# An encoder trunk whose odd mixer gets its weight parts split ahead of time and kept in DRAM scratch

## The chip, the cores and the metric

The kernel runs on one core of a Trainium2 chip. The metric is the device time of one execution in microseconds (us), as the median of several runs. A core has a matrix engine (TensorE, PE in the profile, with its weight loads as PEld), a vector engine (DVE), a scalar engine (ACT), GpSimd (POOL) and a queue that issues DMA transfers (SP). Each engine works through its own instructions strictly in the order in which the program was built; engines wait for each other by semaphores. SBUF is the on-chip memory with 128 partitions, PSUM the small memory that the matrix engine writes, in 8 banks, and DRAM holds inputs, outputs and scratch.

## The reference

Two layers work on x of 512 tokens by 1024 channels, in float32. Each layer is

```
x = x + 1/2 * post1(SwiGLU_1(pre1(x)))
x = x + post2(Mixer(pre2(x)))
x = x + 1/2 * post3(SwiGLU_2(pre3(x)))
```

with RMS norms pre and post, and SwiGLU(h) = (silu(h @ w_gate) * (h @ w_up)) @ w_down with an inner width of 2816. The mixer of layer 0 (the even one) has pooling and windowed attention. The mixer of layer 1 (the odd one) projects h to 4128 columns (od_w_in), runs a convolution of 31 taps over 512 gated channels (the glu pair), a layer norm, a short convolution of 4 taps over 2048 channels (xbc), and a state-space scan in both directions over 16 heads in 4 groups and 4 chunks of 128 tokens; the scan's result is gated by silu(z), normed, joined with the convolution's and projected back (od_w_out).

## The kernel before

The stages run one after the other: feed-forward (0,0), even mixer, feed-forward (0,1), feed-forward (1,0), odd mixer, feed-forward (1,1). Every large product is computed with three matmuls (`mm3`): each operand is given as hi, its rounding to the matmul type fp32r, and lo, the remainder, and hi*hi + hi*lo + lo*hi are added up in a PSUM bank. So each weight has to be split before use.

`Stream` does this for all weights in the order in which they are used. A weight block is some 1 MB, laid out as 128 partitions by 2048 floats; SP loads it into one of 3 buffers (tile `raw`, `RAW_BUFS`). A block has two parts of 128 x 1024. `pump` splits the next part: ACT rounds it into a tile `whi` (line 103), DVE subtracts and writes `wlo` (line 104). whi and wlo are rings of 6 tiles each (`RING`); `get` hands out the next part, `put` gives a ring slot back after its matmuls have been issued and pumps the next split. A raw buffer is loaded again when both its parts are split. A feed-forward stage has 33 blocks: three groups of gate, up and down blocks (names f_g, f_u, f_y in PSUM). The odd mixer has 23: for each of four groups g a block for the gated channels (psum od_ab), one for the scan's B and C (od_bc) and one for the scan's input (od_xs), once a small one for the step sizes (od_dt), four for the gate (od_z), and six of od_w_out (odo_y).

A stage begins with six parts (`first`, `second`): half of the tokens with all six, then the other half, so that the last norm of the stage before can end meanwhile; six ring slots are taken at that time.

In the odd mixer smaller work is woven between the projection's matmuls. DVE computes conv31, 31 instructions for each group (tile `od_ca`, lines 878 and 883), the short convolutions conv4 (`od_cv_B`, `od_cv_C`, `od_cv_x`, line 896), and the chain of the step sizes (`od_dv` to `od_dt`, `od_nacs`, `od_wdec`, `od_rhl`, lines 917 to 970). For each group the scan takes the weighted inputs `od_xw` (line 1007), states `od_st..` (PE) and `od_h` (DVE, lines 1019 and 1020), the scores `od_sc` (PE), their exponentials `od_E` (ACT, line 1046), `od_m` (DVE, lines 1050 and 1051), then `od_yd` and `od_yo` (PE), which DVE adds to `od_y` (lines 1071, 1080, 1082).

What is issued when follows from coroutines with hand-set delays (`Gen.run`), and a scheduling layer below it sets the order of each engine's instructions by its own estimate of when their inputs are ready. So a change of DVE's work in one place can move instructions of any engine.

Of the kernel before, what the change touches and what calls it, by code (L numbers as in the profile page):

```python
# [7 lines left out]
F32 = mybir.dt.float32  # L8
# [4 lines left out]
ALU = mybir.AluOpType  # L13
AX = mybir.AxisListType

P = 128
# [35 lines left out]
LNWAIT = (3500, 2500, 8000)  # L52
SSDWAIT = 2950
CONVWAIT = 5000
DWB, LNG, LNB, CVB, CVW = 0, 4, 8, 12, 28


class Stream:

    def __init__(self, g, blocks):
        self.g = g
        self.blocks = blocks
        self.parts = [(b, j) for b, blk in enumerate(blocks) for j in range(len(blk["parts"]))]
        self.raw, self.done = {}, {}
        self.nraw = self.nsplit = self.pos = 0
        self.live_raw = self.live = 0

    def _load(self, bufs=RAW_BUFS):  # L70
        while self.nraw < len(self.blocks) and self.live_raw < bufs:
            blk = self.blocks[self.nraw]
            t = self.g.raw.tile([P, 2048], F32, tag="raw", name=f"raw{self.nraw}")
            a, b = blk["shape"]
            v = t[:, : a * b].rearrange("p (a b) -> p a b", b=b)
            if self.nraw == 0:
                for h in range(0, b, b // 2):
                    self.g.nc.sync.dma_start(out=v[:, :, h:h + b // 2], in_=blk["src"][:, :, h:h + b // 2])
            elif "srcs" in blk:
                for dst, src in blk["srcs"]:  # L80
                    self.g.nc.sync.dma_start(out=v[dst], in_=src)
            else:
                self.g.nc.sync.dma_start(out=v, in_=blk["src"])
            self.raw[self.nraw] = v
            self.nraw += 1
            self.live_raw += 1

    def pump(self, room=RING):

        g, nc = self.g, self.g.nc  # L90
        self._load()
        while self.nsplit < len(self.parts) and self.live < room:
            b, j = self.parts[self.nsplit]
            if b not in self.raw:
                break
            sl = self.blocks[b]["parts"][j]
            src = self.raw[b][:, sl[0], sl[1]]
            n0, n1 = src.shape[1], src.shape[2]
            h = g.whi.tile([P, 1024], F32R, tag="whi", name=f"whi{self.nsplit}")
            l = g.wlo.tile([P, 1024], F32R, tag="wlo", name=f"wlo{self.nsplit}")  # L100
            hv = h[:, : n0 * n1].rearrange("p (a b) -> p a b", b=n1)
            lv = l[:, : n0 * n1].rearrange("p (a b) -> p a b", b=n1)
            g.later(nc.scalar.copy(out=hv, in_=src), 0)  # L103
            g.later(nc.vector.tensor_tensor(out=lv, in0=src, in1=hv.bitcast(F32), op=ALU.subtract), 1)  # L104
            self.done[self.nsplit] = (hv, lv)
            self.nsplit += 1
            self.live += 1
            if j == len(self.blocks[b]["parts"]) - 1:
                del self.raw[b]
                self.live_raw -= 1  # L110
                self._load()

    def get(self, key):
        b, j = self.parts[self.pos]
        assert self.blocks[b]["key"] == key[:-1] and j == key[-1], (self.blocks[b]["key"], j, key)
        if self.pos not in self.done:
            self.pump()
        r = self.done.pop(self.pos)
        self.pos += 1
        return r  # L120

    def put(self, n=1, pump=True):

        self.live -= n
        if pump:
            self.pump()


def full(n):
    return slice(0, n)  # L130


def ffn_blocks(d, l, i):
    out = []
    f0 = 0
    wg = d["ffn_w_gate"][l, i].rearrange("(k p) f -> p k f", p=P)
    wu = d["ffn_w_up"][l, i].rearrange("(k p) f -> p k f", p=P)
    wd = d["ffn_w_down"][l, i].rearrange("(j p) n -> p j n", p=P)
    for n in FGROUPS:
        for f in range(f0, f0 + n, 2):  # L140
            for nm, w in (("g", wg), ("u", wu)):
                out.append(dict(key=(nm, l, i, f // 2), src=w[:, :, f * P:(f + 2) * P], shape=(KC, 256),
                                parts=[(full(KC), slice(0, 128)), (full(KC), slice(128, 256))]))
        for f in range(f0, f0 + n, 2):
            out.append(dict(key=("d", l, i, f // 2), src=wd[:, f:f + 2, :], shape=(2, 1024),
                            parts=[(slice(0, 1), full(1024)), (slice(1, 2), full(1024))]))
        f0 += n
    return out
# [78 lines left out]
class Gen:  # L227
# [599 lines left out]
    def odd(self):  # L827
# [6 lines left out]
        with ExitStack() as es:  # L834
# [39 lines left out]
            def conv31(g, t):  # L874
# [5 lines left out]
                for i, k in enumerate(k for k in range(31) if k != 15):  # L880
# [4 lines left out]
                    if i % CONVN == CONVN - 1:  # L885
                        yield CONVWAIT

# [362 lines left out]
    def build(self, stages):  # L1250
        nc, tc, d = self.nc, self.tc, self.d
        with ExitStack() as es:
# [11 lines left out]
            self.xl = xp.tile([P, KC, S], F32R, tag="xl", name="xl")  # L1264

            seq = [s for s in ALL if s in stages]
            blocks = []
            for s in seq:
                blocks += ffn_blocks(d, s[1], s[2]) if s[0] == "f" else odd_blocks(d) if s[1] else even_blocks(d)
            self.st = Stream(self, blocks)  # L1270

            def row(s, which):
                l, j = s[1], {"f": (0, 4), "m": (2,)}[s[0]][s[2] if s[0] == "f" else 0] + (which == "post")
# [84 lines left out]
```

## Time and profile before

| | |
|---|---|
| median of 3 runs (lowest to highest) | 2049.24 us (2048.62 to 2052.99) |
| the profiled execution's own time | 2049.17 us |
| its span, first to last instruction | 2047.4 us |
| busy: PE, DVE, ACT, POOL | 2002.0 (98%), 968.1 (47%), 754.3 (37%), 67.7 us (3%) |
| moved by DMA, mean rate | 185.79 MB, 91 GB/s (HBM written 2.10 MB) |
| casts into whi, subtractions into wlo | 329 each, 345.0 us on ACT and 400.9 us on DVE |

The page's own share of PE, 98%, is an average over stages that differ, so the table of stretches below is to be read first. A row of it gives for each engine the busy time within the stretch and the number of instructions in brackets; PEclk is the clock that TensorE was granted, as a share of full speed. In a timeline the brackets at a row's end tell how long the engine had been idle before, and whose result ended that. The last chain is the path of work, followed back from the kernel's end, on which every piece waited for the one before it.

### The profile page before, as it was taken

The numbers are of one execution on the slowest core, as the hardware profiler recorded it, in microseconds if no ns is written. First come the engines' busy times: TensorE is split into PE (matmuls) and PEld (weight loads), VectorE is DVE, ScalarE is ACT, GpSimd is POOL, SyncE is SP. The second block draws the span as 40 slices with busy tenths as digits, with TensorE's granted clock in tenths as the row PEclk, the third lists the DMA queues.
The fourth block names the chain that finished last, engine by engine and source line by source line (L and its number), as shares of the span: only waits on it lengthen the run. The fifth ranks groups of instructions, "written<-read, shape, count | busy, mean of one in ns | idle before, by whom it ended". The sixth has DMA issues, their size and how long they took to land.

```text
span 2047.4 us, 24628 instructions
## 1 busy us (share of the span) xinstructions
PE 2002.0 (98%) x10257; PEld 1693.1 (83%) x10257; DVE 968.1 (47%) x1436; ACT 754.3 (37%) x1242; POOL 67.7 (3%) x94
## 2 busy tenths in 40 slices
PE   8999999999989999999999999998899999999998
PEld 7888888988888888889888888986778889888886
DVE  5323333667453233336323333699898553323334
ACT  5222222576343222224323222465654433232222
POOL 1000000111100000001000000100000010000000
PEclk9999999999999999999999999998899999999999
DMA  7322332330223233322333233232111223233221
GB/s 238 108 88 98 103 100 65 78 100 22 83 96 110 85 101 103 96 89 92 115 103 98 88 103 103 48 106 59 42 62 63 93 71 115 93 103 101 84 83 41
DMA packets 154871, 185.79 MB, mean 91 GB/s; under 512 B 18480, under 2 KB 137864, under 8 KB 154760
## 3 DMA queue, kind: packets, MB, share of 16 engines
q1 hardware_dynamic: 154760, 184.22, 28.7%
q8 instruction: 80, 1.31, 0.3%
q14 instruction: 31, 0.25, 0.0%
HBM read 182.11 MB, written 2.10 MB: 90 GB/s over the span
## 4 chain that ended last, share of the span: by engine, by line
PE 90%; DVE 6%; ACT 2%; POOL 1%; issue 1%; DMA 0%; SPq 0%; POOLq 0%; DVEq 0%; ACTq 0%
PE f_u L299 23%; PE f_g L299 23%; PE f_y L299 23%; PE od_z L299 2%; PE odo_y L299 2%; PE od_bc L299 2%; PE od_ab L299 2%; PE evo_y L299 1%; PE ev_av L299 1%; PE od_xs L299 1%; DVE od_ca L883 1%; PE od_yd L299 1%; PE ev_s L299 1%; PE od_sc L299 1%; PE ev_q L299 1%
## 5 line engine op out<-in xcount | busy, mean ns | idle before, releaser
L103 ACT CAST whi<-raw 128x1024 fp32r<-128x1024 f32 x329 | 345.0, 1052 | 981.2 <-PE f_g L299 323.6
L104 DVE TENSOR_TENSOR wlo<-raw,whi 128x1024 fp32r<-128x1024 f32 x329 | 400.9, 1221 | 630.2 <-ACT whi L103 625.1
L299 PE MATMUL f_g<-xl,whi 128*128 128x512 f32 (+1 forms) x832 | 296.7, 357 | 1.7 <-DVE xl L363 1.4
L299 PE MATMUL f_g<-xh,whi 128*128 128x512 f32 (+1 forms) x832 | 297.2, 357 | 0.6 <-ACT xh L362 0.6
L299 PE MATMUL f_g<-xh,wlo 128*128 128x512 f32 (+1 forms) x832 | 296.4, 356 | 0.0
L299 PE MATMUL f_u<-xh,whi 128*128 128x512 f32 (+1 forms) x768 | 286.5, 373 | 0.2 <-DVE xl L363 0.2
L299 PE MATMUL f_u<-xl,whi 128*128 128x512 f32 (+1 forms) x768 | 286.0, 372 | 0.0
L299 PE MATMUL f_u<-xh,wlo 128*128 128x512 f32 (+1 forms) x768 | 286.0, 372 | 0.0
L299 PE MATMUL f_y<-whi,f_hh 128*128 128x512 f32 x704 | 274.4, 390 | 0.0
L299 PE MATMUL f_y<-whi,f_hl 128*128 128x512 f32 x704 | 273.9, 389 | 0.0
L299 PE MATMUL f_y<-wlo,f_hh 128*128 128x512 f32 x704 | 273.9, 389 | 0.0
L527 DVE TENSOR_TENSOR f_hf<-f_sg,f_u 128x512 f32<-128x512 f32 x88 | 60.6, 689 | 250.5 <-PE f_u L299 249.9
L299 PEld LDWEIGHTS f_g<-xl,whi 128*128 128x128 f32 x832 | 157.2, 189 | 24.9 <-DVE xl L363 1.9
L299 PEld LDWEIGHTS f_g<-xh,whi 128*128 128x128 f32 x832 | 157.2, 189 | 23.8 <-ACT xh L362 1.3
L299 PEld LDWEIGHTS f_g<-xh,wlo 128*128 128x128 f32 x832 | 157.2, 189 | 22.4
L299 PEld LDWEIGHTS f_u<-xh,whi 128*128 128x128 f32 x768 | 145.7, 190 | 25.3 <-DVE xl L363 0.4
L299 PEld LDWEIGHTS f_u<-xl,whi 128*128 128x128 f32 x768 | 145.6, 190 | 24.8
L299 PEld LDWEIGHTS f_u<-xh,wlo 128*128 128x128 f32 x768 | 145.5, 189 | 24.9
L299 PEld LDWEIGHTS f_y<-whi,f_hl 128*128 128x128 f32 x704 | 132.2, 188 | 27.4
L299 PEld LDWEIGHTS f_y<-wlo,f_hh 128*128 128x128 f32 x704 | 132.2, 188 | 27.3
L299 PEld LDWEIGHTS f_y<-whi,f_hh 128*128 128x128 f32 x704 | 132.2, 188 | 27.2
L883 DVE SCALAR_TENSOR_TENSOR od_ca<-od_glu,od_dww,od_ca 128x497 f32<-128x497 f32 (+14 forms) x120 | 88.4, 737 | 0.2
(378 smaller groups left out, 2509.4 us busy)
## 6 DMA issues: line engine op xcount, KB each, us to landing
raw<-ffn_w_up SPq DMA_DIRECT2D x44, 1024.0 KB, 5.3
raw<-ffn_w_down SPq DMA_DIRECT2D x44, 1024.0 KB, 4.9
raw<-ffn_w_gate SPq DMA_DIRECT2D x43, 1024.0 KB, 5.3
raw<-od_w_in SPq DMA_DIRECT2D x16, 512.0 KB, 5.4
raw<-od_w_in SPq DMA_DIRECT2D x8, 1024.0 KB, 5.4
raw<-od_w_out SPq DMA_DIRECT2D x6, 1024.0 KB, 4.9
raw<-ev_w_in SPq DMA_DIRECT2D x3, 1024.0 KB, 5.1
raw<-ev_w_in SPq DMA_DIRECT2D x12, 256.0 KB, 4.5
```

The source lines that it names most:

```text
L103: g.later(nc.scalar.copy(out=hv, in_=src), 0)
L104: g.later(nc.vector.tensor_tensor(out=lv, in0=src, in1=hv.bitcast(F32), op=ALU.subtract), 1)
L299: self.seq(bank, self.nc.tensor.matmul(reg, a, b, start=start, stop=stop, skip_group_check=True))
L527: nc.vector.tensor_tensor(out=h, in0=sg, in1=pu, op=ALU.mult)
L883: V.scalar_tensor_tensor(out=o[:, lo:hi], in0=t[:, lo + sh:hi + sh], scalar=dww[:, k * 4 + g:k * 4 + g + 1], in1=o[:, lo:hi], op0=ALU.mult ...
```

## The change

The blocks of the odd mixer appear twice in the stream now. Their first appearance lies among the feed-forward blocks of the three stages ahead, before the blocks number 6, 9, 13, 16, 19, 22, 25 and 28 of each (`KEEP`; 8, 8 and 7 blocks). There they are loaded and split as any other block, and SP then stores hi and lo of each part into DRAM scratch (tiles k..h and k..l). No matmul uses them there; `_pass` gives their ring slots back as soon as all parts ahead of them have been given back. In the odd mixer, their second appearance, a part needs no raw buffer, no cast and no subtraction: SP loads hi and lo from scratch straight into whi and wlo (line 114 of the new kernel). `_load` skips these blocks, so the raw buffers go on to the blocks of the last feed-forward stage.

```diff
--- before.py
+++ after.py
@@ -52,10 +52,13 @@
 LNWAIT = (3500, 2500, 8000)
 SSDWAIT = 2950
 CONVWAIT = 5000
+KEEP = (6, 9, 13, 16, 19, 22, 25, 28)
 DWB, LNG, LNB, CVB, CVW = 0, 4, 8, 12, 28
 
 
 class Stream:
...
@@ -63,13 +66,16 @@
         self.g = g
         self.blocks = blocks
         self.parts = [(b, j) for b, blk in enumerate(blocks) for j in range(len(blk["parts"]))]
-        self.raw, self.done = {}, {}
-        self.nraw = self.nsplit = self.pos = 0
+        self.raw, self.done, self.kept = {}, {}, {}
+        self.nraw = self.nsplit = self.pos = self.put_to = 0
         self.live_raw = self.live = 0
 
     def _load(self, bufs=RAW_BUFS):
         while self.nraw < len(self.blocks) and self.live_raw < bufs:
             blk = self.blocks[self.nraw]
+            if "split" in blk:
+                self.nraw += 1
+                continue
             t = self.g.raw.tile([P, 2048], F32, tag="raw", name=f"raw{self.nraw}")
             a, b = blk["shape"]
             v = t[:, : a * b].rearrange("p (a b) -> p a b", b=b)
@@ -91,26 +97,46 @@
         self._load()
         while self.nsplit < len(self.parts) and self.live < room:
             b, j = self.parts[self.nsplit]
-            if b not in self.raw:
+            blk = self.blocks[b]
+            if "split" not in blk and b not in self.raw:
                 break
-            sl = self.blocks[b]["parts"][j]
-            src = self.raw[b][:, sl[0], sl[1]]
-            n0, n1 = src.shape[1], src.shape[2]
+            n0, n1 = (sl.stop - sl.start for sl in blk["parts"][j])
             h = g.whi.tile([P, 1024], F32R, tag="whi", name=f"whi{self.nsplit}")
             l = g.wlo.tile([P, 1024], F32R, tag="wlo", name=f"wlo{self.nsplit}")
             hv = h[:, : n0 * n1].rearrange("p (a b) -> p a b", b=n1)
             lv = l[:, : n0 * n1].rearrange("p (a b) -> p a b", b=n1)
-            g.later(nc.scalar.copy(out=hv, in_=src), 0)
-            g.later(nc.vector.tensor_tensor(out=lv, in0=src, in1=hv.bitcast(F32), op=ALU.subtract), 1)
             self.done[self.nsplit] = (hv, lv)
             self.nsplit += 1
             self.live += 1
-            if j == len(self.blocks[b]["parts"]) - 1:
+            last = j == len(blk["parts"]) - 1
+            if "split" in blk:
+                for t, k in zip((h, l), self.kept.pop((blk["key"], j))):
+                    nc.sync.dma_start(out=t[:, :n0 * n1].bitcast(F32), in_=k)
+                continue
+            sl = blk["parts"][j]
+            src = self.raw[b][:, sl[0], sl[1]]
+            g.later(nc.scalar.copy(out=hv, in_=src), 0)
+            g.later(nc.vector.tensor_tensor(out=lv, in0=src, in1=hv.bitcast(F32), op=ALU.subtract), 1)
+            if "keep" in blk:
+                self.kept[blk["key"], j] = [g.keep.tile([P, n0 * n1], F32, tag=f"k{self.nsplit}{x}", name=f"k{self.nsplit}{x}") for x in "hl"]
+                for t, k in zip((h, l), self.kept[blk["key"], j]):
+                    nc.sync.dma_start(out=k, in_=t[:, :n0 * n1].bitcast(F32))
+                self._pass()
+            if last:
                 del self.raw[b]
                 self.live_raw -= 1
                 self._load()
 
+    def _pass(self):
+
+        while self.put_to < self.nsplit and "keep" in self.blocks[self.parts[self.put_to][0]]:
+            self.put_to += 1
+            self.live -= 1
+
     def get(self, key):
+        while "keep" in self.blocks[self.parts[self.pos][0]]:
+            self.done.pop(self.pos, None)
+            self.pos += 1
         b, j = self.parts[self.pos]
         assert self.blocks[b]["key"] == key[:-1] and j == key[-1], (self.blocks[b]["key"], j, key)
         if self.pos not in self.done:
@@ -122,12 +148,27 @@
     def put(self, n=1, pump=True):
 
         self.live -= n
+        self.put_to += n
+        self._pass()
         if pump:
             self.pump()
 
 
 def full(n):
     return slice(0, n)
+
+
+def keep(blocks, ffns):
+
+    todo = list(blocks)
+    for f in ffns:
+        for i in reversed(KEEP[:len(todo)]):
+            f.insert(i, None)
+        for i, b in enumerate(f):
+            if b is None:
+                f[i] = dict(todo.pop(0), keep=True)
+    assert not todo
+    return [dict(b, split=True) for b in blocks]
 
 
 def ffn_blocks(d, l, i):
@@ -1264,10 +1305,10 @@
             self.xl = xp.tile([P, KC, S], F32R, tag="xl", name="xl")
 
             seq = [s for s in ALL if s in stages]
-            blocks = []
-            for s in seq:
-                blocks += ffn_blocks(d, s[1], s[2]) if s[0] == "f" else odd_blocks(d) if s[1] else even_blocks(d)
-            self.st = Stream(self, blocks)
+            lists = {s: ffn_blocks(d, s[1], s[2]) if s[0] == "f" else odd_blocks(d) if s[1] else even_blocks(d) for s in seq}
+            lists["m", 1] = keep(lists["m", 1], [lists[s] for s in seq[:seq.index(("m", 1))] if s[0] == "f"])
+            self.keep = pool("keep", 1, space=bass.MemoryType.DRAM)
+            self.st = Stream(self, [b for s in seq for b in lists[s]])
 
             def row(s, which):
                 l, j = s[1], {"f": (0, 4), "m": (2,)}[s[0]][s[2] if s[0] == "f" else 0] + (which == "post")
```

On DVE, in the odd mixer's first group, around the first od_wdec (it needs od_acs, a product of PE; od_dz and od_dq belong to the step sizes, od_cv_B is a short convolution, od_rhl feeds the scores), there stood:

```order
L952 TENSOR_TENSOR od_wdec<-od_acs 128x128
L896 SCALAR_TENSOR_TENSOR od_cv_B_10625<-od_bc_10592,od_cols,od_cv_B_10625 128x511
L936 TENSOR_TENSOR od_dz<-od_dz,od_de 128x128
L896 SCALAR_TENSOR_TENSOR od_cv_B_10625<-od_bc_10592,od_cols,od_cv_B_10625 128x511
L937 TENSOR_SCALAR od_dq<-od_dz 128x128
L956 TENSOR_TENSOR od_wdec<-od_wdec,od_dt 128x128
L938 RECIPROCAL od_dq<-od_dq 128x128
L970 TENSOR_TENSOR od_rhl_10205<-od_acsh,od_jm 32x512
L939 SCALAR_TENSOR_TENSOR od_dz<-od_dz,od_dq 128x128
L970 TENSOR_TENSOR od_rhl_10205<-od_acsh,od_jm 32x512
L940 SCALAR_TENSOR_TENSOR od_nacs<-od_dz,od_nacs 128x128
```

and there stands now:

```order
L977 TENSOR_TENSOR od_dz<-od_dz,od_de 128x128
L937 SCALAR_TENSOR_TENSOR od_cv_B_11018<-od_bc_10985,od_cols,od_cv_B_11018 128x510
L978 TENSOR_SCALAR od_dq<-od_dz 128x128
L937 SCALAR_TENSOR_TENSOR od_cv_B_11018<-od_bc_10985,od_cols,od_cv_B_11018 128x511
L979 RECIPROCAL od_dq<-od_dq 128x128
L937 SCALAR_TENSOR_TENSOR od_cv_B_11018<-od_bc_10985,od_cols,od_cv_B_11018 128x511
L980 SCALAR_TENSOR_TENSOR od_dz<-od_dz,od_dq 128x128
L993 TENSOR_TENSOR od_wdec<-od_acs 128x128
L981 SCALAR_TENSOR_TENSOR od_nacs<-od_dz,od_nacs 128x128
L1011 TENSOR_TENSOR od_rhl_10611<-od_acsh,od_jm 32x512 x2
L1011 TENSOR_TENSOR od_rhl_10612<-od_acsh,od_jm 32x512 x2
L924 SCALAR_TENSOR_TENSOR od_ca_10585<-od_glu_10983,od_dww,od_ca_10585 128x498
```

The reciprocal and its neighbours, and the convolution steps, have moved ahead of od_wdec; the wlo that stood three rows ahead of it is gone.

On DVE, a little later, from the first od_y that adds an od_yd (first chunk of the first group) on, there stood:

```order
L1071 TENSOR_TENSOR od_y<-od_y,od_yd_10820 128x256
L883 SCALAR_TENSOR_TENSOR od_ca_10178<-od_glu_10267,od_dww,od_ca_10178 128x498
L1050 TENSOR_TENSOR od_m_10803<-od_E_10798,od_E_10793 128x512
L883 SCALAR_TENSOR_TENSOR od_ca_10178<-od_glu_10267,od_dww,od_ca_10178 128x497
L1051 TENSOR_TENSOR od_m_10803<-od_m_10803,od_cb_10540 128x512
L1082 TENSOR_TENSOR od_y<-od_y,od_yo_10830 128x256
L104 TENSOR_TENSOR wlo_10835<-raw_10440,whi_10834 128x1024
L896 SCALAR_TENSOR_TENSOR od_cv_x_10840<-od_xs_10736,od_cols,od_cv_x_10840 128x510
L878 TENSOR_SCALAR od_ca_10179<-od_glu_10590,od_dww,od_cols 128x512
L896 SCALAR_TENSOR_TENSOR od_cv_x_10840<-od_xs_10736,od_cols,od_cv_x_10840 128x511
L883 SCALAR_TENSOR_TENSOR od_ca_10179<-od_glu_10590,od_dww,od_ca_10179 128x497
L896 SCALAR_TENSOR_TENSOR od_cv_x_10840<-od_xs_10736,od_cols,od_cv_x_10840 128x511
```

and there stands now:

```order
L1112 TENSOR_TENSOR od_y<-od_y,od_yd_11210 128x256
L937 SCALAR_TENSOR_TENSOR od_cv_x_11228<-od_xs_11126,od_cols,od_cv_x_11228 128x511
L1123 TENSOR_TENSOR od_y<-od_y,od_yo_11220 128x256
L1060 TENSOR_TENSOR od_h_11283<-od_h_11213,od_etot 128x256
L924 SCALAR_TENSOR_TENSOR od_ca_10585<-od_glu_10983,od_dww,od_ca_10585 128x502
L1061 TENSOR_TENSOR od_h_11283<-od_h_11283,od_yd_11280 128x256
L924 SCALAR_TENSOR_TENSOR od_ca_10585<-od_glu_10983,od_dww,od_ca_10585 128x503
L1091 TENSOR_TENSOR od_m_11193<-od_E_11188,od_E_11183 128x512
L1121 TENSOR_TENSOR od_yo_11291<-od_yo_11281,od_eacs 128x512
L1092 TENSOR_TENSOR od_m_11193<-od_m_11193,od_cb_10936 128x512
L924 SCALAR_TENSOR_TENSOR od_ca_10585<-od_glu_10983,od_dww,od_ca_10585 128x504
L1060 TENSOR_TENSOR od_h_11346<-od_h_11283,od_etot 128x256
```

A wlo and several od_ca have left; od_h and the next chunks' od_m have come nearer to the od_y. A second wlo, 15 rows further on, is gone too.

On SP, at the end of feed-forward (1,0), where the odd mixer's first weights are fetched (raw from od_w_in; k.. are scratch tiles), there stood:

```order
L83 DMA raw_9335<-ffn_w_down 128x2x1024
L83 DMA raw_9403<-ffn_w_down 128x2x1024
L83 DMA raw_9471<-ffn_w_down 128x2x1024
L81 DMA raw_9539<-od_w_in 128x8x128 x2
L81 DMA raw_9608<-od_w_in 128x8x128 x2
L83 DMA raw_9677<-od_w_in 128x8x256
L83 DMA raw_9898<-od_w_in 128x8x32
L81 DMA raw_9977<-od_w_in 128x8x128 x2
L81 DMA raw_9988<-od_w_in 128x8x128 x2
L845 DMA od_pb<-ssm_dt_bias 128x32
```

and there stands now:

```order
L89 DMA raw_9887<-ffn_w_down 128x2x1024
L89 DMA raw_9955<-ffn_w_gate 128x8x256
L89 DMA raw_10023<-ffn_w_up 128x8x256
L89 DMA raw_10091<-ffn_w_gate 128x8x256
L114 DMA wlo_10299<-k13l 128x1024
L114 DMA whi_10298<-k13h 128x1024
L114 DMA whi_10308<-k14h 128x1024
L114 DMA wlo_10309<-k14l 128x1024
L114 DMA whi_10318<-k21h 128x1024
L114 DMA wlo_10319<-k21l 128x1024
L114 DMA whi_10385<-k22h 128x1024
L114 DMA wlo_10386<-k22l 128x1024
```

The three raw buffers take blocks of feed-forward (1,1), and behind them come the loads of hi and lo, two for each part.

## Rows read from the trace of the kernel before

**Rows 1.** by stretch, us: feed-forward block (1,0), odd mixer's middle. Columns: first row.

```profile
core 0: us, PE busy (x) PEld busy (x) DVE busy (x) ACT busy (x) POOL busy (x), PEclk, DMA share, GB/s
...
942.00:1307.00 365.00, 365.00 (x1765) 308.72 (x1764) 140.62 (x165) 111.30 (x152) 7.34 (x9) 1.00 0.31 98
...
1350.00:1580.00 230.00, 213.52 (x1078) 172.71 (x1076) 209.49 (x368) 132.65 (x261) 0.00 (x0) 0.93 0.20 60
```

**Rows 2.** timeline of PE, odd mixer: start, us, ..., [idle before, released by].

```profile
1389.08 1.21 PE L299 MATMUL od_st0a<-od_xw,od_bt 128*128 128x256 f32 x2 [3.96 <-DVE od_xw L1007]
...
1420.60 3.65 PE L299 MATMUL od_yd<-od_xt,od_m 128*128 128x64 f32 x16 [3.87 <-DVE od_m L1051]
...
1464.08 1.87 PE L299 MATMUL od_yd<-od_xt,od_m 128*128 128x64 f32 x8 [2.49 <-DVE od_h L1020]
...
1468.59 1.97 PE L299 MATMUL od_yd<-od_xt,od_m 128*128 128x64 f32 x8 [2.65 <-DVE od_m L1051]
...
1531.13 0.66 PE L314 MATMUL od_tp<-ident,od_cv_x 128*128 128x128 f32 x4 [2.23 <-ACT od_cv_x L903]
...
1565.10 1.10 PE L299 MATMUL od_yd<-od_xt,od_m 128*128 128x64 f32 x8 [1.26 <-DVE od_h L1020]
...
1581.56 1.05 PE L299 MATMUL od_var<-ones,od_csq 128*128 128x1 f32 x8 [1.33 <-ACT od_csq L1184]
```

**Rows 3.** by stretch: the stretches of low granted clock in the odd mixer.

```profile
1389.00:1400.00 11.00, 10.92 (x24) 6.02 (x24) 10.04 (x18) 7.74 (x15) 0.00 (x0) 0.53 0.00 0
1420.00:1427.00 7.00, 6.40 (x24) 5.84 (x25) 5.61 (x12) 1.48 (x2) 0.00 (x0) 0.52 0.01 2
1532.00:1536.00 4.00, 4.00 (x24) 4.00 (x23) 4.00 (x8) 2.30 (x5) 0.00 (x0) 0.57 0.02 4
1566.00:1570.00 4.00, 4.00 (x21) 3.95 (x21) 4.00 (x10) 0.63 (x1) 0.00 (x0) 0.58 0.00 0
1583.00:1591.00 8.00, 8.00 (x45) 8.00 (x44) 1.32 (x2) 1.62 (x3) 0.55 (x1) 0.57 0.00 1
```

**Rows 4.** by stretch: the odd mixer's middle, instructions with tile wlo alone.

```profile
1350.00:1600.00 250.00, 92.19 (x261) 52.17 (x260) 27.64 (x23) 0.92 0.18 55
```

**Rows 5.** the page's groups by line: busy, mean ns | idle before.

```profile
L103 ACT CAST whi<-raw 128x1024 fp32r<-128x1024 f32 x329 | 345.0, 1052 | 981.2 <-PE f_g L299 323.6
```

**Rows 6.** timeline of DVE, odd mixer, same columns as rows 2.

```profile
1371.11 0.28 DVE L952 TENSOR_TENSOR od_wdec<-od_acs 128x128 f32<-128x128 f32 x1
...
1388.08 0.95 DVE L1007 TENSOR_TENSOR od_xw<-od_xt,od_wdec 128x768 f32<-128x768 f32 x1
...
1402.28 0.42 DVE L1071 TENSOR_TENSOR od_y<-od_y,od_yd 128x256 f32<-128x256 f32 x1 [2.02 <-PE od_yd L299]
...
1419.77 0.68 DVE L1051 TENSOR_TENSOR od_m<-od_m,od_cb 128x512 f32<-128x512 f32 x1
```

**Rows 7.** the chain that ended last, odd mixer: start, us, what.

```profile
1307.00 5.75 PE od_ab L299 x48
...
1321.68 4.31 PE od_xs L299 x36
...
1378.71 1.14 DVE wlo L104
...
1402.70 0.65 DVE od_ca L883
...
1525.56 1.13 DVE wlo L104
```

**Rows 8.** timeline of ACT, end of the block before the odd mixer.

```profile
1299.34 1.05 ACT L103 CAST whi<-raw 128x1024 fp32r<-128x1024 f32 x1
```

**Rows 9.** by stretch: the kernel's start, when DMA queues are full.

```profile
14.00:34.00 20.00, 19.86 (x167) 19.87 (x168) 11.92 (x15) 9.39 (x15) 1.45 (x3) 1.00 0.97 323
```

**Rows 10.** the page's DMA issues: KB each, us from issue to landing.

```profile
raw<-ffn_w_down SPq DMA_DIRECT2D x44, 1024.0 KB, 4.9
...
out<-x SPq DMA_DIRECT2D x3, 512.0 KB, 2.6
```

## The prediction

> **What bounds the kernel now.** I read the stretches by engine first. In a feed-forward block TensorE (PE) is busy for 365.00 of 365.00 us at full clock, with DVE at 141 and ACT at 111 us [rows 1]: nothing done on DVE or ACT there can shorten it, and there is room on both. In the middle of the odd mixer, 1350 to 1580 us, the picture turns: DVE is busy for 209.5 of 230 us, PE for 213.5, and the granted clock is 0.93 [rows 1]. There PE waits. Its timeline has seven stalls, all at small matmuls that need a result of DVE, in two cases by way of ACT: 3.96, 3.87, 2.49, 2.65, 2.23, 1.26 and 1.33 us, 17.8 in sum [rows 2]. I call them A, B, C1, C2, D, E and F. After A, B, D, E and F come some us at the lower of the two clock levels (1.2 instead of 2.4 GHz). What that costs is busy time times the missing share of the clock: 10.92 x 0.47 = 5.1 us after A, 6.40 x 0.48 = 3.1 after B, 4.00 x 0.43 = 1.7 after D, 4.00 x 0.42 = 1.7 after E, 8.00 x 0.43 = 3.4 after F [rows 3]. So by these rows the odd mixer could give back 17.8 + 15.0 = 33 us at most, and a split has a share in what keeps DVE busy: 23 instructions that write wlo, 27.6 us, between 1350 and 1600 [rows 4].
>
> **What it removes.** 23 blocks of the odd mixer are 45 parts (the dt block has one). Their 45 casts on ACT (1.05 us, [rows 5]) and 45 subtractions on DVE (27.64 / 23 = 1.20 us, [rows 4]) leave the odd mixer and go into the first three feed-forward blocks, 15 parts to each. DVE there goes from 141 to 159 and ACT from 111 to 127 us of 365 [rows 1]. I cost this at nothing: the ring still holds four ready parts while two kept ones stand in it, and a part is worth 365 / 66 = 5.5 us of PE (33 blocks of two parts, [rows 1]), so PE has 22 us of work in hand, against 2.3 us for a split and 7 us for the three splits that follow when a kept pair is passed. Without that cover each kept block would cost up to 7 us, and there are 23.
>
> **What it adds on the queue.** SP gets 90 stores of up to 512 KB and 90 loads. Per kept block that is 1 MB read and 2 MB written beside three ordinary blocks. A store of 512 KB lands in 2.6 us and a load of 1 MB in 4.9 [rows 10], so even one after the other this is 4 x 2.6 + 4 x 4.9 = 30 us in the 33.2 us that PE needs for three blocks (365 / 11); with the queue full it moved 323 GB/s [rows 9], by which 6 MB take 19.5 us. SP stands still at a store until both halves of the split are done, and the raw loads queue behind it; but the raw load behind waited for that same subtraction before, so only the stores' own time is new to it.
>
> **The start of the odd mixer** is the tight place. A ready raw block in SBUF is replaced by a load that can be issued only when a ring slot is free. The first slot comes free at about 1299.3 [rows 8], and the other five within the next 8 us. By the single landing of 4.9 us the first part is there at 1304.2, and by 323 GB/s (1.05 MB in 3.25 us) the sixth at 1320.5. PE wants the first at 1307.0 and the sixth at 1321.68 + 12 x 0.12 = 1323.1 [rows 7], so every part is 2 to 3 us early and I take 0. The other end: if each load waited for the landing of the one before, the sixth would come at 1299.3 + 6 x 4.9 = 1328.7, 5.6 us late. The trace has no load from DRAM scratch; its rows of 4 KB are those of the down-projection blocks, hence 4.9.
> The Trainium skill (DMA: Bandwidth & Descriptors, section Bandwidth) speaks against the change here: it wants transfers of at least 1 MiB and measures 6.15 us for one, and each part is now two of half that size. By that figure, one after the other, the sixth part would be 13 us late; by the row of the full queue, where transfers of 512 KB and 1 MB overlapped, it is in time.
> Later loads have a slot six parts ahead, 30 us and more, and I cost them at nothing.
>
> **What the freed DVE time is worth.** The scheduler has ordered DVE anew, so I go stall by stall with the new order.
> A: PE waits for od_xw. In DVE's order 28 rows stand from od_wdec to od_xw, 17.9 us [rows 6]; now there are 16. Gone from between are one wlo (1.14, [rows 7]), three taps and three convolution steps of 0.65 [rows 7], the reciprocal with its three short neighbours (about 1.7) and an idle 0.6: 7.3 us. They now stand ahead of od_wdec. DVE arrives there earlier by the two wlo before it, less two more taps, about 1.1, and has about 4.9 us more to do before od_wdec, so 3.8 are paid back and od_xw comes 3.5 earlier. PE reaches its od_st0a five od_xs matmuls earlier (5 x 0.24 = 1.2) and does them afterwards, so 2.3 us are gained and 1.7 of idle stay. The low clock after it I expect to last like that after E and F (1.7 and 3.4, mean 2.5) instead of 5.1: another 2.6. Sum 4.9.
> B: PE waits for the last od_m. From the first od_y to it DVE works 18.2 us almost without a pause [rows 6]. In the new order two wlo (2.3), five taps and two convolution steps (4.6) have left this piece and three short rows (at most 1.5) have come into it: 12.8 us. That is 5.4 less for a stall of 3.87. But three times DVE must now wait inside the piece for a od_yd that PE has just got its od_m for. I take 3.0 of the stall and half of the clock loss, 1.6: 4.6.
> C1: one wlo of 1.13 stands in its chain; 1.1. C2 has none and stays.
> D: three wlo, 3.4 us, stand in the chain up to the last convolution; the first and the last of the seven on the whole chain are in [rows 7]. The stall of 2.23 goes with its 1.7 of low clock: 3.9.
> E and F: no wlo in E's chain, and F hangs on the mean and variance of the convolution. 0.
> Sum: 4.9 + 4.6 + 1.1 + 3.9 = 14.5. What is late next is C2.
> The profiled execution took 2049.17 us (span 2047.4 and 1.8 around it), which is the median of the runs (2049.24) for this purpose. Forecast: 2049.2 - 14.5 = 2034.7, say 2035.
>
> **Rivals.**
> 1. Only what is on the chain goes. The new order shifts waits rather than removing them, low clock included, and just the seven wlo on the chain count, capped by the stalls: 1.1 (A) + 2.3 (B) + 1.1 (C1) + 2.2 (D) = 6.8. Time 2042. For it: stalls as short as 1.3 us were followed by low clock too [rows 2, 3]. Against: DVE's pieces get shorter by more than their wlo.
> 2. All stalls and the low clock after them vanish, 33 us: 2016. For it: DVE would lose 27.6 of 209.5 us [rows 1, 4]. Against: C2, E and F have no wlo in their chains.
> 3. The first loads of the odd mixer do not overlap. Then PE waits 5.6 us there and pays a low clock like A's, 5.1: 2035 + 11 = 2046. This is where the page's rule would show; against it stands [rows 9].
> 4. No change. PE's static order now puts od_yd and od_st0a earlier; if DVE is late for them, PE stands earlier with the od_ab or od_xs matmuls queued behind, and the wait only changes place: 2049.
> 5. Slower: kept blocks starve the feed-forward blocks. Four stores and a raw load lie before the next raw block on SP. If stores were as slow as the loads, 4 x 4.9 + 4.9 = 24.5 us against the 22.1 us (two blocks of 11.06) that the raw buffers hide, PE would wait 2.4 us for each kept block, 23 times: 55 us. From 0.63 us per kept block on the gain of 14.5 is eaten; at 1 us the time is 2035 + 23 = 2058. For it: the trace holds only 2 MB of stores, at its end, and none beside loads. Against: they landed in 2.6 us [rows 10], and the DMA engines are busy for only 0.31 there [rows 1].
>
> **How the numbers follow.** Forecast 0.53 (its own range 2028 to 2042), rival 1 0.12, rival 2 0.08, rival 3 0.08, rival 4 0.09, rival 5 0.10. A measurement of this kernel tells no change from one within 0.2%, 4.1 us, so faster is below 2045.1 and slower above 2053.3. Faster: 0.53 + 0.12 + 0.08 and 0.03 of rival 3, 0.76; same: the rest of it and rival 4, 0.14; slower 0.10. The range 2020 to 2048 leaves out rival 2 and rival 5 and a little of rival 4.
>
> **What would show it.** Right: no cast or subtraction with raw between the odd mixer's first and last matmul, the PE timeline without the waits B and D, A under 2 us, C2 still at 2.6; the mean clock of 1350 to 1570 up from 0.93 to 0.95 or more; feed-forward blocks still 365 us; no PE wait for whi or wlo at the first od_ab, od_bc and od_xs. Wrong: PE waiting for a DMA into whi or wlo (rival 3), a feed-forward block over 366 us (rival 5), stalls of the same sum in other places of the odd mixer (rival 4).

## The result and the profile after

The changed kernel takes 2015.62 us (median of 4 runs, 2014.79 to 2016.45), against 2050.05 for the kernel before beside it: ratio 0.983 (95% interval 0.9813 to 0.9847), 34 us faster. The forecast was 2035 with a range of 2020 to 2048; the time lies below it, and the gain is 2.4 times the one forecast. (One execution of lo_only, below, took 6435.25 us, for which no trace shows a reason; its figures are those of its other three.)

All of it is in the odd mixer. I measure that stage from the first od_ab matmul to the first f_g of the next stage in PE's timeline: 1306.83 to 1676.21 us before, 369.4 us; 1308.37 to 1643.33 after, 335.0 us. The last feed-forward block takes 371.3 us, before 371.2. The 1.5 us by which the mixer begins later were lost in the first 28 us of the kernel; in the kernels below it begins between 1301 and 1309.

The same two stretches as [rows 1], from the profile after (columns as there):

```profile
942.00:1307.00 365.00, 365.00 (x1764) 308.63 (x1763) 154.38 (x176) 122.90 (x162) 6.30 (x9) 1.00 0.48 163
1350.00:1580.00 230.00, 227.88 (x1290) 189.38 (x1289) 197.01 (x370) 130.53 (x268) 2.77 (x4) 1.00 0.37 129
```

The feed-forward block holds PE at 365.00 of 365.00 us with 13.8 us more on DVE, 11.6 on ACT and half as much DMA again. In the mixer PE went from 213.5 to 227.9 us busy, and the clock from 0.93 to 1.00. DVE is still busy for 197 of 230 us, since it now reaches later work within the stretch (370 instructions without the splits, 368 with them before).

What PE waited for from 1300 to 1650 us after (who, for what: us in total, times, longest), in place of the seven stalls of [rows 2]:

```profile
PE od_yd L340 <- DVE od_m L1092: 1.3, 2, 1.1
PE ody_tp L355 <- DVE od_yl L404: 0.8, 1, 0.8
PE f_g L340 <- ACT xh L403: 0.4, 1, 0.4
PE f_g L340 <- DVE odo_p_m L430: 0.3, 1, 0.3
```

A, B, D, E and F are gone; of C1 and C2, 5.1 us together, 1.12 are left at C2's place. The od_m and ody_tp rows are what remains in the stage; the last two rows stood there before as well. Over the whole stage PE's idle time went from 18.7 to 2.5 us, and its busy time, for the same matmuls, from 350.6 to 332.5. So of the 34.4 us about 16 are idle time and the other 18 the low clock, which is gone throughout (0.94 before, 1.00 now).

The start of the odd mixer, which I had called the tight place (the answers to [rows 9], and then one load of the sixth part: KB, us to landing):

```profile
1300.00:1310.00 10.00, 10.00 (x56) 8.64 (x55) 6.11 (x11) 2.88 (x7) 1.10 (x2) 1.00 0.80 288
1310.00:1320.00 10.00, 10.00 (x86) 10.00 (x85) 5.17 (x9) 2.49 (x6) 1.10 (x2) 1.00 0.86 345
...
whi<-k32h SPq DMA_DIRECT2D x1, 512.0 KB, 10.2
```

A load took up to 10.2 us, but twelve were issued between 1300.65 and 1310.03, so that they overlapped and moved 288 and 345 GB/s together, and PE waited for none. The Trainium skill (DMA: Bandwidth & Descriptors, section Bandwidth) gives 6.15 us for a transfer of 1 MB, issued there from GpSimd; by an estimate from it, loads one after the other would be late. Here the size of one did not decide.

SP's waits at the stores (line 123), whole execution:

```profile
SPq L123 <- ACT whi L118: 137.4, 45, 3.9
...
SPq L123 <- DVE wlo L119: 49.3, 44, 1.8
```

89 waits of 2.1 us on average, 3.9 at most, while the raw buffers hide 22 us: nobody starved.

### The profile page after: what moved, and what is told of

The parts are those of the page before. It is cut to its first block, busy times and chain, and to the rows that moved or that the text cites. A ratio compares the mean times of both kernels' runs of the same rounds, so it can differ in the third digit from the quotient of the medians.

```text
span 2014.6 us, 25022 instructions
## 1 busy us (share of the span) xinstructions
PE 1985.5 (99%) x10257; PEld 1681.7 (83%) x10257; DVE 970.7 (48%) x1436; ACT 761.9 (38%) x1246; POOL 65.7 (3%) x94
## 4 chain that ended last, share of the span: by engine, by line
PE 93%; DVE 3%; ACT 2%; POOL 1%; issue 1%; DMA 0%; SPq 0%; POOLq 0%; DVEq 0%; ACTq 0%
PE f_g L340 24%; PE f_u L340 24%; PE f_y L340 24%; PE od_ab L340 2%; PE od_bc L340 2%; PE od_xs L340 2%; PE odo_y L340 2%; PE od_z L340 2%; PE evo_y L340 1%; PE ev_av L340 1%; PE od_sc L340 1%; PE ev_s L340 1%; PE od_yd L340 1%; PE ev_q L340 1%; PE ev_pT L355 1%
```

## The experiments

Two things changed in the odd mixer together: DVE has 45 x 1.2 = 54 us less to do, and the scheduling layer, which sees that, orders DVE and PE anew. (Within the stage DVE's busy time fell by 45.5 us, from 288.5 to 243.0.) Counted over the 432 DVE instructions of the stage that both kernels have, 1558 pairs of them stand the other way round. order_before, order_after, both_before and both_after hold the order and change the time. The stage's length is read like the 369.4 and 335.0 above, from the one profiled execution of each kernel, so how long the clock happened to stay low in that execution counts in it.

**order_before, order_after.** A chain of order-only dependencies over the DVE instructions of the stage (`seen` holds them as the program issues them, `ORDER` the place of each):

```diff
+ORDER = (
...
             self.run(main())
+            for p, q in zip(ORDER, ORDER[1:]):
+                tc.add_manual_dep(self.seen[ORDER_AT + q], self.seen[ORDER_AT + p].name, mybir.DependencyInfo(
+                    mybir.DependencyClass.NoSync, mybir.DependencyReason.DATA), reason="order")
```

> The changed kernel, but DVE's instructions of the odd mixer (all but the subtractions, which are gone from it) are held in the order that they had before the change. Theory T (DVE was the queue that everything in the odd mixer waited in, and taking 54 us of subtractions out of it shortens the queue at every place, whatever the order): 2015 to 2023 us, the seven stalls gone or under 1 us. Rival O (most of the gain is the scheduler's new order of DVE's work): 2033 to 2045 us, with stalls A, B, C2, E and F largely as before.

> The kernel before, with all its subtractions in the odd mixer, but DVE's other instructions held in the order of the changed kernel. T: 2044 to 2056 us, since DVE has as much to do as before. O: 2016 to 2032 us.

Measured 2042.33 us (ratio 0.9962, 0.9948 to 0.9976) and 2052.16 us (1.0015, 1.0006 to 1.0024). My theory T fell in the first: with the old order the freed time brought 8 us, not 34. Its rival O fell in the second: the new order of DVE alone brought nothing. PE's order was left to the scheduler in both, so neither verdict is clean yet.

**lo_only, hi_only.** One half of each part is kept and loaded; for the other half the raw block is loaded again in the mixer and ACT casts, or DVE subtracts. In lo_only, among other lines:

```diff
+            kept = self.kept.pop((blk["key"], j)) if "split" in blk else None
             g.later(nc.scalar.copy(out=hv, in_=src), 0)
-            g.later(nc.vector.tensor_tensor(out=lv, in0=src, in1=hv.bitcast(F32), op=ALU.subtract), 1)
+            if kept is not None:
+                nc.sync.dma_start(out=l[:, :n0 * n1].bitcast(F32), in_=kept)
+            else:
+                g.later(nc.vector.tensor_tensor(out=lv, in0=src, in1=hv.bitcast(F32), op=ALU.subtract), 1)
```

> Only lo is kept in scratch and loaded; the odd mixer loads the raw blocks too, and ACT casts them to hi there as before. T: 2014 to 2019 us, as the changed kernel, because DVE's time alone counts. Rival A (ACT's 47 us of casts were part of the waits, since D and F were released by ACT): 2022 to 2038 us, with waits for ACT left in the odd mixer.

> Only hi is kept in scratch and loaded; the odd mixer loads the raw blocks too, and DVE subtracts there as before, so ACT alone is relieved. T: 2044 to 2052 us, the stalls of before. A: 2020 to 2038 us.

Measured 2018.22 (0.9843, 0.9826 to 0.9859) and 2052.82 us (1.001, 1.000 to 1.002). Relieving ACT alone brings nothing, relieving DVE alone nearly all. In these two the scheduler chose the order itself, and with DVE's time it chose nearly that of the changed kernel (271 pairs from it), without it nearly that of before (90 pairs).

**both_before, both_after.** order_before could have been slow because PE's order did not fit. So the same chain, on PE's matmuls from the first od_ab to the first odo_y too.

> The changed kernel with the order of before held in the odd mixer on DVE and on PE (in order_before PE's order was the scheduler's, neither that of before nor that of the changed kernel). Theory Q (the freed time is worth its full 34 us only together with the order that the scheduler makes from it, because in the old order DVE stands at an od_y that waits for PE while the od_m that PE waits for is queued behind it): 2036 to 2046 us, B and C2 as before. Theory T (time alone counts, and order_before was slow only because its PE and DVE orders didn't fit each other): 2015 to 2026 us.

> The kernel before, with all its subtractions and casts, but DVE and PE held in the order of the changed kernel in the odd mixer. Q and T: 2044 to 2058 us, the order alone is worth nothing or costs, since DVE comes late to everything. O (the new order by itself gives the gain, and order_after failed only by PE's order): 2016 to 2035 us.

Measured 2039.20 (0.9937, 0.9920 to 0.9954) and 2040.10 us (0.9947, 0.9932 to 0.9962). T fell in both. both_before lies where Q put it; both_after lies between the forecasts, faster than Q and T said and slower than O said, so the order alone is worth something, but not the whole gain. The stage's length, us, with PE's idle time and mean clock in it:

| | old order | new order |
|---|---|---|
| DVE splits in the stage | 369.4 (before; idle 18.7, clock 0.94) | 359.4 (both_after; idle 17.2, clock 0.98) |
| DVE does not | 362.5 (both_before; idle 14.5, clock 0.95) | 335.0 (after; idle 2.5, clock 1.00) |

In these executions the freed time alone is worth 6.9 us, the order alone 10.0 (nearly all of it clock, not idle time), both 34.4: 17.5 us come only from the two together. The 6.9 are the low end: the profiled execution of both_before is the longest of its four (2035.60 to 2042.26 us). Up to F it was 9.8 us ahead of the kernel before, and it lost 2.9 again behind F, where its clock stayed low longer (the rows are in the last section). By the medians of all executions the three are 11.4, 10.5 and 34.4 us, and 12.5 come only from both.

PE's stalls in both_before (timeline, columns as in [rows 2]):

```profile
1386.88 0.70 PE L307 MATMUL od_st0a<-od_xw,od_bt 128*128 128x256 f32 x2 [1.86 <-DVE od_xw L307]
...
1414.33 1.94 PE L307 MATMUL od_yd<-od_xt,od_m 128*128 128x64 f32 x8 [3.86 <-DVE od_m L307]
...
1457.93 1.10 PE L307 MATMUL od_yd<-od_xt,od_m 128*128 128x64 f32 x8 [1.35 <-DVE od_h L307]
...
1461.68 1.97 PE L307 MATMUL od_yd<-od_xt,od_m 128*128 128x64 f32 x8 [2.65 <-DVE od_m L307]
...
1522.66 0.66 PE L307 MATMUL od_tp<-ident,od_cv_x 128*128 128x128 f32 x4 [0.76 <-ACT od_cv_x L997]
...
1555.13 1.10 PE L307 MATMUL od_yd<-od_xt,od_m 128*128 128x64 f32 x8 [1.26 <-DVE od_h L307]
...
1571.65 1.05 PE L307 MATMUL od_var<-ones,od_csq 128*128 128x1 f32 x8 [1.33 <-ACT od_csq L1278]
```

Line by line against [rows 2]: A, C1 and D got shorter by 2.1, 1.1 and 1.5 us, but B, C2, E and F have the length of before to 0.01 us, though DVE has 54 us less to do. These four are set by the order, not by how much DVE has to do: with the old order less work does not shorten them, and with the new order and all the work (both_after, below) B, E and F are gone, but for 0.78 us at an od_mean, and 1.11 of C2 are left. What that looks like on DVE at B, in both_before:

```profile
1409.59 0.42 DVE L307 TENSOR_TENSOR od_y<-od_y,od_yd 128x256 f32<-128x256 f32 x1 [0.99 <-PE od_yd L307]
1409.92 0.74 DVE L307 SCALAR_TENSOR_TENSOR od_ca<-od_glu,od_dww,od_ca 128x502 f32<-128x502 f32 x1
...
1412.55 0.69 DVE L307 TENSOR_TENSOR od_m<-od_E,od_E 128x512 f32<-128x512 f32 x1
1413.16 0.42 DVE L307 TENSOR_TENSOR od_h<-od_h,od_etot 128x256 f32<-128x256 f32 x1
1413.49 0.69 DVE L307 TENSOR_TENSOR od_m<-od_m,od_cb 128x512 f32<-128x512 f32 x1
1414.09 0.42 DVE L307 TENSOR_TENSOR od_h<-od_h,od_yd 128x256 f32<-128x256 f32 x1
```

DVE itself waits for PE at the od_y; behind it stand three taps and two additions of od_y, then the od_m that PE's next od_yd needs. PE waits for DVE from its od_yo on, until 1414.18. An earlier DVE only waits longer at the od_y: 0.99 us here, none in the kernel before, where a wlo ran until then. (The Trainium skill, PSUM — Partial Sum Buffer, section Engine vs sequencer instructions, calls VectorE's queue strict FIFO; this trace agrees, the od_m did not pass the waiting od_y.)

In both_after it is the other way: no stall over 1.2 us at an od_yd, but DVE, with its old load, is late for the chain of the step sizes and for the short convolutions:

```profile
1357.29 0.66 PE L265 MATMUL od_tp<-ident,od_cv_x 128*128 128x128 f32 x4 [1.84 <-ACT od_cv_x L955]
...
1377.82 1.12 PE L265 MATMUL od_acs<-od_dv,od_tri 128*128 128x64 f32 x4 [5.36 <-DVE od_dv L265]
...
1396.16 0.70 PE L265 MATMUL od_st0a<-od_xw,od_bt 128*128 128x256 f32 x2 [0.91 <-DVE od_xw L265]
...
1464.09 1.10 PE L265 MATMUL od_yd<-od_xt,od_m 128*128 128x64 f32 x8 [1.11 <-DVE od_m L265]
...
1525.96 0.66 PE L265 MATMUL od_tp<-ident,od_cv_x 128*128 128x128 f32 x4 [1.95 <-ACT od_cv_x L955]
```

**dve_back, dve_half.** After each pair of loads (dve_half is shown; dve_back takes all n1 columns):

```diff
                     nc.sync.dma_start(out=t[:, :n0 * n1].bitcast(F32), in_=k)
+                v = lv[:, :, :n1 // 2]
+                nc.vector.tensor_tensor(out=v, in0=v.bitcast(F32), in1=v.bitcast(F32), op=ALU.max)
                 continue
```

> The changed kernel, where each of the 45 loaded lo parts is passed once through DVE again (elementwise maximum with itself, 128 x 1024, in place), so that DVE's time of before is back and the scheduler, who sees it, makes nearly the order of before. Q and T: 2046 to 2056 us. A theory in which ACT's relief or the loads themselves bring the gain: 2016 to 2035 us.

> As dve_back, but on half of the columns of each part, so that about half of DVE's 54 us comes back. T (time alone, in proportion): 2030 to 2036 us. Q: the order that the scheduler makes from this stands nearer to that of before, so more than half of the gain is lost: 2037 to 2048 us.

Measured 2054.54 (1.0021, 1.0012 to 1.0030) and 2034.82 us (0.9921, 0.9896 to 0.9946); stage 373.8 and 350.0 us. With DVE's time back the whole gain goes, so neither the loads nor ACT made it. Half of it (DVE is busy for 25 of the 45.5 us again) costs some half of the gain, as T had forecast: Q's price was wrong here, the scheduler's order (436 pairs from that of before) is worth something on the way too. It is no closer than that: two executions of dve_half took 2030 us, the profiled one among them, and two 2039.

**groups, tail.** `odd[:13]` or `odd[13:]` alone goes through `keep`.

> Only the 13 blocks of the odd mixer's four groups (25 of the 45 parts) are split early; the z and od_w_out blocks (20 parts) are split in the odd mixer as before. If the gain goes by DVE's time taken out, in proportion to the parts: 34 x 25 / 45 = 19, 2031 us. Theory S (time and order each give some 10 us and the rest comes only where both are there, so it goes by place: A to C lie among these parts, and the order made for them is close to that of the changed kernel; D, E and F come where the z parts are split again): A to C gone with their low clock, 22 to 27 us, so 2023 to 2029 us, and a stall or two left after 1500 us.

> The reverse: only the z and od_w_out blocks (20 parts) are split early, the 25 parts of the groups in the odd mixer as before. In proportion: 34 x 20 / 45 = 15, 2035 us. S: A to C stay, D to F go with their low clock (4.8 + 6.8 us at most), 2038 to 2045 us.

Measured 2026.81 (0.9889, 0.9872 to 0.9905) and 2036.99 us (0.9942, 0.9927 to 0.9956); the stage is 21.4 and 11.3 us shorter, 32.7 of 34.4 in sum. PE's stalls after 1500 us in groups, and all until then in tail:

```profile
1507.72 0.65 PE L355 MATMUL od_tp<-ident,od_cv_x 128*128 128x128 f32 x4 [0.77 <-ACT od_cv_x L944]
1540.88 1.18 PE L340 MATMUL od_yd<-od_xt,od_m 128*128 128x64 f32 x8 [1.80 <-DVE od_h L1061]
1557.41 1.05 PE L340 MATMUL od_var<-ones,od_csq 128*128 128x1 f32 x8 [1.33 <-ACT od_csq L1225]
```

```profile
1387.78 1.22 PE L340 MATMUL od_st0a<-od_xw,od_bt 128*128 128x256 f32 x2 [3.97 <-DVE od_xw L1048]
1419.24 1.09 PE L340 MATMUL od_yd<-od_xt,od_m 128*128 128x64 f32 x4 [3.87 <-DVE od_m L1092]
1462.67 1.91 PE L340 MATMUL od_yd<-od_xt,od_m 128*128 128x64 f32 x8 [2.49 <-DVE od_h L1061]
1467.23 1.97 PE L340 MATMUL od_yd<-od_xt,od_m 128*128 128x64 f32 x8 [2.65 <-DVE od_m L1092]
```

The gain goes by place, as theory S has it: in tail A to C stand as before and D to F are gone; in groups A and B are gone and 1.1 us of C is left, F stands, E has grown to 1.80, and of D 0.77 is left. DVE's busy time in the stage fell by nearly the same in both, 23.5 and 22.3 us, and the gain is 21.4 in one and 11.3 in the other. By the whole time groups lies in the range of S, tail between the two forecasts.

**fix_late, fix_early, fix2_late, fix2_early.** Is it a few rows that make such a stall? In both_before, and in the kernel before held in its own order, the rows at B are put otherwise. In fix_late (one line each here; DVE's numbers in order of issue: 117 is the od_y that waits, 125 and 126 the fourth chunk's od_m), and then in fix2_late (127 and 128 are the third chunk's od_h):

```diff
-118, 116, 121, 117, 122, 119, 123, 120, 124, 125, 127, 126, 128, 130,
+118, 116, 121, 125, 126, 117, 122, 119, 123, 120, 124, 127, 128, 130,
...
+118, 116, 121, 127, 128, 125, 126, 117, 122, 119, 123, 120, 124, 130,
```

On PE all four put the third chunk's od_yd ahead of the fourth's.

> both_before (the changed kernel in the old order of DVE and PE) with two places put otherwise, both at stall B: DVE makes the last od_m of the first group ahead of the od_y that adds the second chunk's od_yd instead of 9 rows behind it, and PE does the third chunk's od_yd before the fourth's. If B, which stayed at 3.86 us with the freed time, is made by these rows alone: B and the low clock after it go, 2039 - 7 = 2032 us (2029 to 2035), C2, E and F stay as they are. If B hangs on something else: B stays over 2.5 us, 2037 to 2042 us.

> The kernel before in its own order, with all its subtractions, and the same two places put otherwise. If the rows alone make B: 2050 - 7 = 2043 us (2041 to 2046). If B needs the freed time too (a subtraction of 1.2 us stands right ahead of that od_y): B keeps 1.5 us or more and the low clock after it, 2046 to 2051 us.

Measured 2044.18 (0.9970, 0.9959 to 0.9981) and 2052.16 us (1.0010, 1.0001 to 1.0019): no gain in either. B moved to another row, in fix_late:

```profile
1415.47 3.67 PE L307 MATMUL od_yd<-od_xt,od_m 128*128 128x64 f32 x16 [4.41 <-DVE od_h L307]
```

> fix_late with one more pair of rows put forward on DVE. In fix_late B was 4.41 us and released by the od_h of the third chunk: PE's od_yd of that chunk shares its PSUM bank with the state product that this od_h reads, and od_h stood 12 rows behind the od_y. Now DVE makes that od_h (two rows) and the last od_m (two rows) ahead of the od_y. If these rows make B: B under 1 us, no low clock after it, 2039 - 7 = 2032 us (2029 to 2036), the other stalls as in both_before. If another row takes their place once more: B over 2.5 us, 2038 to 2045 us.

> The kernel before in its own order, with all its subtractions, and the same rows of fix2_late put forward. If the rows alone make B: 2050 - 7 = 2043 us (2040 to 2046). If B needs the freed time too (two subtractions stand between the first od_y and that place): B keeps 1.3 us or more with the low clock after it, 2046 to 2051 us.

fix2_late: 2036.46 us (0.9935, 0.9919 to 0.9952), half a us above the range expected; the stage 355.4 us, 7.1 less than both_before. The stretch with B in both_before and in fix2_late:

```profile
1400.00:1430.00 30.00, 26.14 (x117) 21.36 (x116) 24.68 (x46) 13.44 (x29) 0.00 (x0) 0.83 0.24 73
```

```profile
1400.00:1430.00 30.00, 29.12 (x147) 23.22 (x146) 28.66 (x54) 17.30 (x39) 0.00 (x0) 1.00 0.30 105
```

PE idled 3.9 us and ran at 0.83; now 0.9 and full clock, which is 3.0 of idle and 26.14 x 0.17 = 4.4 of clock. Four DVE rows and the order of two products made stall B; whether the products' order is needed was not tried by itself. What that is worth in time is not shown: the 7.1 us agree with the 7 expected by luck, since fix2_late lost some 3 us of clock at A and gained some 3 behind F, where nothing was moved. By the medians the two runs differ by 2.7 us, both spread by 6, and their intervals lie on each other. fix2_early: 2049.48 us (0.9996, 0.9986 to 1.0006). With the subtractions in place the same rows cut B from 3.87 to 1.09 us, and the stage is 369.2 us, as before: C2 grew to 3.15, PE's idle time over the stage fell by 1.4 us only (18.7 to 17.4), and its busy time for the same matmuls grew by 1.2 (350.6 to 351.8).

**f01_too, even_too.** What the changed kernel still waits for longest after its start is the norm at the even mixer's end. Six more parts (and in even_too those of the even mixer) are split early:

```diff
...
+            nxt = lists["f", 0, 1]
+            for i, b in zip(EARLY, nxt[:3]):
+                lists["f", 0, 0].insert(i, dict(b, keep=True))
+            nxt[:3] = [dict(b, split=True) for b in nxt[:3]]
...
```

> The changed kernel, and the first three blocks (six parts) of feed-forward (0,1) are split early in feed-forward (0,0) as well. At the end of the even mixer the changed kernel's PE waits 4.05 us for the last norm on DVE, where four subtractions of 1.2 us stand, and the granted clock is 0.83 for the next 20 us. If these subtractions are what the norm is late by: 2009 to 2013 us, against 2015 to 2017 for the changed kernel. If the chain of the norm itself sets the end (ACT, POOL and DVE by turns, 0.6 to 1.3 us a piece): no change, 2014 to 2018 us.

> As f01_too, and all 13 blocks of the even mixer are split early in feed-forward (0,0), those of the odd mixer in the next two stages alone (12 and 11 blocks). The even mixer's waits for ACT (1.30 and 1.68 us) may go too: 2005 to 2012 us. If the first stage cannot hold 16 kept blocks (stores and raw loads in one queue), PE waits there for whi or wlo and it is slower than f01_too, 2014 to 2030 us.

Measured 2011.98 (0.9817, 0.9802 to 0.9832) and 2009.81 us (0.9806, 0.9792 to 0.9821), with the odd mixer unchanged at 334.9 us. Every execution of both was shorter than every one of the changed kernel (2014.27 at most against 2014.79 at least), though the intervals of the ratios overlap. The stretch behind that norm, after and f01_too:

```profile
580.00:600.00 20.00, 15.95 (x115) 15.78 (x114) 6.40 (x8) 3.40 (x6) 1.95 (x2) 0.83 0.28 92
```

```profile
580.00:600.00 20.00, 19.20 (x161) 19.23 (x162) 5.60 (x7) 4.98 (x6) 0.00 (x0) 1.00 0.00 1
```

The wait went from 4.05 to 2.60 us, and the clock stayed up in this execution, the shortest of four. even_too leaves 2.52 there, with a clock of 0.83 from 578 to 588 us, and cuts the even mixer's waits for ACT from 1.30 and 1.68 to 0.69 and 0.45; that it beats f01_too is not settled, their intervals overlap.

## Why the prediction was wrong

- **The feed-forward blocks cost nothing**: right, 365.00 of 365.00 us at clock 1.00; rival 5 did not happen.
- **The start of the odd mixer costs nothing**: right, no wait for whi or wlo; rival 3 did not happen.
- **D, 3.9**: right, 2.23 and its low clock are gone. With the old order held, the freed time alone cut it to 0.76 and the clock behind it was 1.00.
- **A, 4.9 and B, 4.6**: right in kind, too small. Of A all 3.96 + 5.1 = 9.1 went, of B all 3.87 + 3.1 = 7.0. The piece from od_wdec to od_xw got 7.2 us shorter, as I had said (7.3), but od_wdec came only 1.9 us later in the stage, not 3.8, so od_xw came 5.3 us earlier, not 3.5. B's piece went from 18.2 to 13.8 us, which was enough for all of the stall. And half of the low clock was left standing by assumption, for A by a figure taken from E and F, which vanished too.
- **C1 1.1, C2 0, E 0 and F 0**: the step that failed. "No wlo in its chain" was read truly: with the old order held, C2, E and F kept their length to 0.01 us. But from it I concluded that they stay. The change also moved the order, I had read the new order for A and B alone, and the order is what made these waits. C gave 4.0 us of idle and 3.9 of low clock, E 3.0 with its own, F 4.7: 15.6 us, for which I had taken 1.1. C's low clock I had overlooked altogether; in the kernel before it is 8.27 x 0.47 = 3.9 us:

```profile
1464.00:1475.00 11.00, 8.27 (x28) 7.14 (x29) 8.57 (x17) 1.91 (x2) 0.00 (x0) 0.53 0.33 95
```

- **The sum**: with C's clock the seven stalls and the low clock behind them are 36.7 us, not the "33 us at most" that I had called the limit, and the gain, 34.4, lies above that limit. Of the signs, "C2 still at 2.6" failed; it is 1.12.
- **Which rival it was**: 2016 of rival 2 is the time, held at 0.08, and outside the range. Against it I had put the very sentence that failed. That it is right to the microsecond is luck: C's clock was missing from its 33 us, and 1.9 us of idle are left or new (1.12 and 0.80). Rival 4, a wait that only changes place, is what the freed time meets where the order stays: in order_before and both_before B was untouched and DVE waited for PE at the od_y.

By the runs, of the 34.4 us: 7 to 11 from time that the old order could use, 10 from the order even without it, 12 to 18 from both together. Which rows of the order make C2, E and F was not tried; only for B were rows moved.

## What to carry to other kernels

When work leaves an engine whose order a scheduler sets, read the new order at every stall, also at those that the removed work does not touch: a wait in which two in-order engines wait for each other by turns, as B here, got no shorter by freed time, and went when the right rows were moved (the first choice of rows only moved it). To price time and order apart, hold the order with order-only dependencies and change the time, and the reverse; neither half need be worth much alone. And where each stall was followed by some us of low clock, the stalls that went took them along: half was too cautious. A stage read from one execution holds that execution's low clock too, so it is set beside the times of all.

## What the hardware showed unasked

A stall of 1.12 us (C2's rest, after) had no low clock behind it, the granted clock from 1450 to 1460 us is 1.00; those of 1.26 and 1.33 us, E and F before, had 4 and 8 us of it [rows 3]. But behind the 1.11 us at 1464.09 in both_after the clock was 0.83 from 1465 to 1475 us. Nor does one and the same wait always cost the same. A (1.86 us) and F (1.33 us) are as long in fix2_late as in both_before, and the rows around them stand in the same order. Behind A and behind F, in both_before:

```profile
1386.88:1400.00 13.12, 12.75 (x55) 8.57 (x55) 11.89 (x21) 11.62 (x29) 0.00 (x0) 1.00 0.15 61
1571.00:1591.00 20.00, 19.35 (x111) 19.23 (x112) 7.64 (x18) 4.40 (x9) 2.22 (x3) 0.66 0.00 1
```

and in fix2_late:

```profile
1385.88:1399.00 13.12, 13.12 (x43) 8.08 (x44) 10.44 (x19) 10.69 (x24) 0.00 (x0) 0.74 0.16 64
1566.00:1586.00 20.00, 19.35 (x137) 19.23 (x138) 9.84 (x21) 6.56 (x11) 2.22 (x3) 0.83 0.04 4
```

A cost no clock in the one and 13.12 x 0.26 = 3.4 us in the other. Behind F the kernel before has 0.83 over 20 us (1581 to 1601) as well. The four executions of both_before differ in the same way: two had a mean clock of 0.992 and took 2035.60 and 2037.01 us, two had 0.989 and took 2041.38 and 2042.26. Length alone does not tell which stall costs clock; what does is not shown.
